# Rotating images by 90 degrees: one queue with all loads before all stores, larger load packets, and a slab parked in PSUM

## The chip, the cores and the metric

One core of a Trainium2 chip; the other cores are idle. The metric is device time in microseconds (us) of one execution, as the median of several runs. The spread of a kernel's runs is mostly 0.1 to 0.3%, and the verdict of "faster" or "slower" asks for 2%.

Ratios are the mean time of one kernel's fast runs over the mean time of the other's fast runs of the same rounds on the same chip, so they are not quite the ratio of the medians that are quoted beside them.

## The reference

A batch of 32 images with 3 channels, each plane 256 x 256 in fp32, is turned clockwise by 90 degrees. Nothing is computed: 25.17 MB go in, 25.17 MB come out.

```python
def setup_inputs():
    batch, c, h, w = 32, 3, 256, 256
    return {"x": np.random.randn(batch, c, h, w).astype(np.float32)}

def reference(x):
    return np.rot90(x, k=-1, axes=(-2, -1)).astype(np.float32)
```

## The kernel before

The 96 planes are cut into 24 slabs of 1 MB (4 planes). A partition holds 8 rows of a plane, which are 8 KB in one piece of memory. VectorE transposes blocks of 32 x 32; the access patterns put the reversed rows in their places. SyncE issues the loads, ScalarE the stores, each on its own DMA queue. Twelve input and twelve output buffers let both run at once. The first two stores are cut into packets of 2 KB, all other packets have 8 KB (a packet is what has a record of its own in the trace: a load of 1 MB in rows of 8 KB has 128 of them, a store of 1 MB in pieces of 2 KB has 512).

```python
    R = 8
    G = H // R
    n_slabs = B * C * G // P
    SHORT = 2
    ld_v = x.rearrange("b c h w -> (b c h) w").rearrange("(n p r) w -> n p (r w)", p=P, r=R)
    st_v = out.rearrange("b c h w -> (b c h) w").rearrange("(n p c) w -> n p (c w)", p=P, c=R)
    # ... pools of 12 buffers each ...
    for n in range(n_slabs):
        t_in = in_pool.tile([P, R * W], fp32, tag="t_in")
        nc.sync.dma_start(out=t_in, in_=ld_v[n])
        t_out = out_pool.tile([P, R * W], fp32, tag="t_out")
        src = t_in.rearrange("p (r g c) -> p c r g", r=R, c=R)
        dst = t_out.rearrange("p (c g r) -> p c r g", c=R, r=R)[:, :, ::-1, ::-1]
        parts = 2 if n in (0, n_slabs - 1) else 1
        for k in range(parts):
            cs = slice(k * R // parts, (k + 1) * R // parts)
            nc.vector.transpose(out=dst[:, cs], in_=src[:, cs])
        nc.scalar.dma_start(out=st_v[n], in_=t_out,
                            max_dma_last_dim=2048 if n < SHORT else 8192)
```

## Time and profile before

| | before |
|---|---|
| time | 124.11 us (124.02 to 124.44, 3 runs); with the later rounds 124.23 us (6 runs) |
| span in the profile | 122.4 us |
| bytes moved by DMA | 50.33 MB |
| first to last data packet | 119.4 us |
| VectorE busy | 91.6 us |

The lines of the page. The first gives busy us, share of the span and instructions of each engine. "DVE" (VectorE) and "DMA" give the busy share in tenths for 40 equal slices, "GB/s" the bytes moved in each slice.
```profile
DVE 91.6 (75%) x26; POOL 0.2 (0%) x4
...
DVE  0199999999999999999999999697796793000000
...
DMA  2999999999999999999999999999999999999994
GB/s 83 426 428 428 390 428 424 422 421 426 424 428 418 428 426 420 426 428 428 426 428 428 428 428 428 428 426 426 428 428 428 426 428 428 428 428 426 428 428 193
```

DMA is at 9 from the second slice to the last but one, and moves 420 to 428 GB/s nearly always: DMA bounds the kernel. VectorE does nothing in the last six slices.

The table by stretches (stretch in us from the start of the span, its length, busy us of VectorE and GpSimd with their instructions, clock of TensorE, busy share of DMA, GB/s):

```profile
core 0: us, DVE busy (x) POOL busy (x), PEclk, DMA share, GB/s
...
4.00:9.00 5.00, 3.35 (x2) 0.00 (x0) 1.00 1.01 428
...
12.00:15.00 3.00, 3.00 (x2) 0.00 (x0) 1.00 1.02 399
...
40.00:56.00 16.00, 16.00 (x5) 0.00 (x0) 1.00 1.01 427
...
59.00:63.00 4.00, 4.00 (x2) 0.00 (x0) 1.00 1.01 426
...
98.00:120.00 22.00, 3.98 (x2) 0.00 (x0) 1.00 1.01 428
```

From 4 to 9 us there are only loads, from 40 to 56 us loads and stores mixed, from 98 to 120 us only stores: 427 or 428 GB/s for all three.

The main group of VectorE's transpositions (line, engine, operation, tiles, shapes, count, then busy us and mean ns of one, then idle time before them and what ended it), and its last two in the timeline (start, us, ...):

```profile
L53 DVE STREAM_TRANSPOSE t_out<-t_in 128x2048 f32<-128x2048 f32 x22 | 83.8, 3936 | 3.8 <-DMA t_in<-in_x_dram 3.8
```

```profile
98.08 3.98 DVE L53 STREAM_TRANSPOSE t_out<-t_in 128x1024 f32<-128x1024 f32 x2 [0.99 <-DMA t_in<-in_x_dram]
```

A transposition of 2048 elements per partition takes 3.94 us. The last ends at 102.1 us, 20 us before the end of the span.

The trace also has a record of each DMA packet. Of these I use the time that a packet took, and the mean distance of packet starts on one engine, worked out from bytes and rate:

```
packet    took      start to start
 8 KB     309 ns    306.6 ns  (427.5 GB/s over 16 engines)
 2 KB      84 ns     81 ns
```

### The profile page before, as it was taken

What the parts mean: (1) busy time and instruction counts of PE and PEld (TensorE: products, weight loads), DVE (VectorE), ACT (ScalarE), POOL (GpSimd) and SP (SyncE); (2) the same over time, 40 slices, a digit from 0 to 9 for tenths busy, and PEclk for the clock granted to TensorE, in tenths of its full rate; (3) what the DMA queues carried; (4) which work ended last, traced back from release to release, by engine and by line L of the source; (5) the groups of instructions that cost most, each with busy time, mean ns of one, the idle gap of its engine ahead of it and who ended that gap; (6) DMA issues with size and microseconds to landing.
All of it is one profiled execution on the core that took longest, in us unless ns stands there. A gap on an engine that the chain in (4) does not pass through costs nothing.

```text
span 122.4 us, 164 instructions
## 1 busy us (share of the span) xinstructions
DVE 91.6 (75%) x26; POOL 0.2 (0%) x4
## 2 busy tenths in 40 slices
DVE  0199999999999999999999999697796793000000
POOL 0000000000000000000000000000000000000000
DMA  2999999999999999999999999999999999999994
GB/s 83 426 428 428 390 428 424 422 421 426 424 428 418 428 426 420 426 428 428 426 428 428 428 428 428 428 426 426 428 428 428 426 428 428 428 428 426 428 428 193
DMA packets 7680, 50.33 MB, mean 411 GB/s; under 512 B 768, under 2 KB 768, under 8 KB 1792
## 3 DMA queue, kind: packets, MB, share of 16 engines
q1 hardware_dynamic: 3456, 25.17, 49.1%
q10 hardware_dynamic: 4224, 25.17, 49.0%
HBM read 25.17 MB, written 25.17 MB: 411 GB/s over the span
## 4 chain that ended last, share of the span: by engine, by line
DMA 78%; DVE 2%; DVEq 2%; SPq 1%; issue 0%
DMA t_in<-in_x_dram 78%; DVE t_out L53 2%; DVEq L82 2%; SPq L45 1%; DVEq L53 0%
## 5 line engine op out<-in xcount | busy, mean ns | idle before, releaser
L53 DVE STREAM_TRANSPOSE t_out<-t_in 128x2048 f32<-128x2048 f32 (+1 forms) x26 | 91.6, 3647 | 10.4 <-DMA t_in<-in_x_dram 10.4
L71 POOL MEMSET const-bfloat16-1.0<- 128x1 bf16 x1 | 0.1, 102 | 0.0
L71 POOL MEMSET const-uint8-127<- 128x1 uint8 x1 | 0.1, 102 | 0.0
L71 POOL MEMSET const-float32-0.0<- 128x1 f32 x1 | 0.1, 99 | 0.2 <-issue 0.2
L71 POOL MEMSET const-float32-1.0<- 128x1 f32 x1 | 0.1, 99 | 0.0
## 6 DMA issues: line engine op xcount, KB each, us to landing
t_in<-in_x_dram SPq DMA_DIRECT2D x24, 1024.0 KB, 14.4
out_dram<-t_out ACTq DMA_DIRECT2D x24, 1024.0 KB, 19.5
```

The source lines that it names most:

```text
L45: nc.sync.dma_start(out=t_in, in_=ld_v[n])
L53: nc.vector.transpose(out=dst[:, cs], in_=src[:, cs])
L71: nc = _bacc.Bacc("TRN2", target_bir_lowering=False, num_devices=1)
L82: with _tile.TileContext(nc) as tc:
```

## The change

The intent: fewer and larger load packets, one queue that first loads everything and then stores everything, and no buffers beyond the input itself. Twelve units of 2 MB in SBUF hold the whole input (16 KB per partition each). Slab n, turned, goes into the unit that slab n-1 has left; slab 0 goes into PSUM and is copied into the last unit by ScalarE when all is turned. In slabs 1 to 10 a partition holds 16 rows (16 KB in one piece); a load fills every second partition with the first four planes of the slab, a second load the others. Slab 1's store is split into 128 KB (1 KB packets), 896 KB (7 KB packets) and 1 MB.

```diff
+    RI, RO = 16, 8
+    K = H // RI
+    I = 2
+    Q = P // (K * I)
     # ...
+    ld8_v = rows_in.rearrange("(n i p r) w -> n p i (r w)", i=I, p=P, r=RO)
+    ld16_v = rows_in.rearrange("(n i m r) w -> n i m (r w)", i=I, m=Q * K, r=RI)
+    st_v = rows_out.rearrange("(n i p c) w -> n p i (c w)", i=I, p=P, c=RO)
     # ...
     for n in range(n_slabs):
-        t_in = in_pool.tile([P, R * W], fp32, tag="t_in")
-        nc.sync.dma_start(out=t_in, in_=ld_v[n])
+        if n == last:
+            nc.sync.dma_start(out=units[n], in_=ld8_v[n])
+            continue
+        for i in range(I):
+            if n == 0:
+                nc.sync.dma_start(out=units[n][:, i], in_=ld8_v[n][:, i])
+            else:
+                nc.sync.dma_start(out=units[n][i::I].rearrange("p i f -> p (i f)"), in_=ld16_v[n, i])
     # ...
+    for n in range(n_slabs):
+        t_in, t_out = units[n], units[n - 1] if n else turned0
     # ... slabs 0 and 11 are turned as before, the others so:
+            src = t_in.rearrange("p i f -> p (i f)").rearrange("p (r g c) -> p c r g", r=RI, c=RO)
+            dst = t_out.rearrange("p i (c k r) -> p c r k i", c=RO, r=RI)[:, :, ::-1, ::-1, :]
+            for h in range(2):
+                cs = slice(h * RO // 2, (h + 1) * RO // 2)
+                nc.vector.transpose(out=dst[:, cs], in_=src[:, cs])
-        nc.scalar.dma_start(out=st_v[n], in_=t_out,
-                            max_dma_last_dim=2048 if n < SHORT else 8192)
+        if n == 1:
+            nc.sync.dma_start(out=st_v[n][:, 0, :W], in_=t_out[:, 0, :W])
+            nc.sync.dma_start(out=st_v[n][:, 0, W:], in_=t_out[:, 0, W:])
+            nc.sync.dma_start(out=st_v[n][:, 1], in_=t_out[:, 1])
+        elif n:
+            nc.sync.dma_start(out=st_v[n], in_=t_out)
+    for i in range(I):
+        nc.scalar.copy(out=units[last][:, i], in_=turned0[:, i])
+    nc.sync.dma_start(out=st_v[0], in_=units[last])
```

More of the change, by code (lines that the diff above doesn't have):

```diff
@@ L31 @@
     P = nc.NUM_PARTITIONS
-    R = 8
-    G = H // R
-    n_slabs = B * C * G // P
-    SHORT = 2
-    ld_v = x.rearrange("b c h w -> (b c h) w").rearrange("(n p r) w -> n p (r w)", p=P, r=R)
-    st_v = out.rearrange("b c h w -> (b c h) w").rearrange("(n p c) w -> n p (c w)", p=P, c=R)
-    in_pool = ctx.enter_context(tc.tile_pool(name="in_pool", bufs=12))
-    out_pool = ctx.enter_context(tc.tile_pool(name="out_pool", bufs=12))
-    for n in range(n_slabs):
-        t_in = in_pool.tile([P, R * W], fp32, tag="t_in")
-        nc.sync.dma_start(out=t_in, in_=ld_v[n])
-        t_out = out_pool.tile([P, R * W], fp32, tag="t_out")
-        src = t_in.rearrange("p (r g c) -> p c r g", r=R, c=R)
-        dst = t_out.rearrange("p (c g r) -> p c r g", c=R, r=R)[:, :, ::-1, ::-1]
-        parts = 2 if n in (0, n_slabs - 1) else 1
-        for k in range(parts):
-            cs = slice(k * R // parts, (k + 1) * R // parts)
-            nc.vector.transpose(out=dst[:, cs], in_=src[:, cs])
-        nc.scalar.dma_start(out=st_v[n], in_=t_out,
-                            max_dma_last_dim=2048 if n < SHORT else 8192)
+    RI, RO = 16, 8
@@ new lines @@
+    K = H // RI
+    I = 2
+    Q = P // (K * I)
+    n_slabs = B * C // (Q * I)
+    last = n_slabs - 1
+    F = RO * W
+    rows_in = x.rearrange("b c h w -> (b c h) w")
+    rows_out = out.rearrange("b c h w -> (b c h) w")
+    ld8_v = rows_in.rearrange("(n i p r) w -> n p i (r w)", i=I, p=P, r=RO)
+    ld16_v = rows_in.rearrange("(n i m r) w -> n i m (r w)", i=I, m=Q * K, r=RI)
+    st_v = rows_out.rearrange("(n i p c) w -> n p i (c w)", i=I, p=P, c=RO)
+    pools = [ctx.enter_context(tc.tile_pool(name=f"unit{u}", bufs=1)) for u in range(n_slabs)]
@@ new lines @@
+    units = [pool.tile([P, I, F], fp32, name=f"u{u}") for u, pool in enumerate(pools)]
+    psum = ctx.enter_context(tc.tile_pool(name="psum", bufs=1, space=bass.MemoryType.PSUM))
+    turned0 = psum.tile([P, I, F], fp32, name="turned0")
+    for n in range(n_slabs):
+        if n == last:
[6 more added lines that the diff above has]
+                nc.sync.dma_start(out=units[n][i::I].rearrange("p i f -> p (i f)"), in_=ld16_v[n, i])
@@ new lines @@
+    for n in range(n_slabs):
+        t_in, t_out = units[n], units[n - 1] if n else turned0
+        if n in (0, last):
+            for i in range(I):
+                src = t_in[:, i].rearrange("p (r g c) -> p c r g", r=RO, c=RO)
+                dst = t_out[:, i].rearrange("p (c g r) -> p c r g", c=RO, r=RO)
+                nc.vector.transpose(out=dst[:, :, ::-1, ::-1], in_=src)
+        else:
+            src = t_in.rearrange("p i f -> p (i f)").rearrange("p (r g c) -> p c r g", r=RI, c=RO)
[9 more added lines that the diff above has]
+            nc.sync.dma_start(out=st_v[n], in_=t_out)
@@ L60 @@
+    for i in range(I):
+        nc.scalar.copy(out=units[last][:, i], in_=turned0[:, i])
+    nc.sync.dma_start(out=st_v[0], in_=units[last])
 _INS = ['x']
```

## The prediction

> **What bounds the kernel now.** The DMA engines. In the page's slices they are 90% busy or more from the second slice to the second last, mostly at 428 GB/s; the table by stretches gives 428 GB/s for 4 to 9 us (loads only), 40 to 95 us (mixed) and 98 to 120 us (stores only): direction and mixing cost nothing. 50.33 MB at 428 GB/s is 117.6 us of the 122.4 us span. The rest is 2 us before the first packet, slow first packets (307 GB/s from 2 to 4 us), the final drain, and 14 to 34 us at 423 GB/s. VectorE is busy 91.6 us and not the limit: DMA stores for 20 us after its last transposition (102 us).
>
> **What a packet costs.** In the trace's packet records an 8 KB packet takes 309 ns (306.6 ns start to start per engine), a 2 KB packet 84 ns (about 81). The line through both is 36.7 ns per KB plus 5.8 ns per packet.[...]
>
> **What the change does to DMA.**
> - 20 of 24 MB of loads go from 8 KB to 16 KB packets: 80 fewer per engine, x 5.8 ns = 0.46 us saved.
> - Two stores leave 2 KB packets: 48 fewer per engine, 0.28 us saved. One store split into 1 KB and 7 KB: 0.05 us lost.
> - Bytes, start and drain stay. Separating loads from stores saves nothing.
> Sum: 0.7 us, all on the critical path.
>
> **What it does to VectorE.** 24 pieces of 3.94 us remain: 94.5 us from 5.7 us on, so it ends near 101 us; two ScalarE copies from PSUM follow[...]. Loads end near 60 us; slab n (2 MB, 4.9 us) is stored from 60 + 4.9(n-1), and turned by 5.7 + 7.9(n+1). Slab 1: turned at 21 us, wanted at 60; slab 11: 101 and 109; slab 0: copied by 104, wanted at 114. VectorE stays hidden, by about 8 us, unless a piece grows by over 9%. One queue suffices: an issue takes 0.4 us against 2.4 us of transfer.
>
> **Predicted: 123.4 us, range 122.4 to 125.2.** Faster by over 2%: 0.05; within 2%: 0.81; slower by over 2%: 0.14.
>
> **What would show each step.** 16 KB packets near 607 ns start to start, loads at 431 GB/s; stores at 427 to 428; DMA at 9 in all slices, no gap near 60 us. Transpositions near 3.9 us, the last done by 102 us, none late in the chain of waits.
>
> **What would make it wrong.**
> 1. Loads go to every second partition, 64 at a time.[...] No run shows it yet.
> 2. Turned elements are written alternately 8 KB apart, and slab 0 into PSUM. If a piece takes over 4.3 us, the last slabs are late for their stores, DMA idles near 105 us, and the time grows by about 0.95 us per further 1%.
> 3. The turn from loads to stores in one queue leaves a bubble of over 1 us.
> A gain over 2% would need the ends (4 us) to shrink, which nothing here does.

0.46 + 0.28 - 0.05 is about 0.7 us, each from the 5.8 ns per packet that its line through the 8 KB and 2 KB packets gives (80, 48 and 8 packets). The 104 us for slab 0 rests on a guess of mine for the time of a copy from PSUM; it took 1.87 us.

## The result, and the profile after

| | before | after |
|---|---|---|
| time | 124.23 us (124.0 to 124.44, 6 runs) | 123.98 us (123.92 to 124.17, 6 runs) |
| ratio | | 0.9983, 95% interval 0.9967 to 0.9998 |
| span in the profile | 122.4 us | 122.2 us |
| first to last data packet | 119.43 us | 119.08 us |

The same kernel run again as a control on the chip of the first experiments gave 123.96 us, ratio 0.9976 (0.9964 to 0.9988). So the gain is 0.2 to 0.3 us, where 0.7 us was forecast. The time lies inside the stated range; the change is "within 2%", as forecast; but the gain is about a third of its forecast size. The stated range is 2.8 us wide and holds the time of the kernel before as well, so that it was met says little.

The same lines of the page, after:

```profile
DVE 93.3 (76%) x24; ACT 5.0 (4%) x3; POOL 0.2 (0%) x4
...
DVE  0299999999999999999999999999999940000000
...
DMA  3999999999999999999999999999999999999993
GB/s 88 429 432 434 440 440 429 429 429 429 429 429 429 429 429 424 434 424 408 370 414 428 426 429 429 429 429 429 429 429 429 424 429 429 429 429 426 429 429 166
```

DMA is at 9 throughout here too, and over a quarter of the packets is gone (the page counts 7680 before, 5584 after). The slices that matter are the 19th to 21st: 408, 370, 414 GB/s. They lie at 55 to 64 us, where the one queue turns from loads to stores.

The table by stretches (now with a column for ScalarE). Rates of short stretches wobble where packets are 16 KB (436 GB/s from 4 to 9 us, 419 from 9 to 14 us), so that 436 is not a rate above the others:

```profile
core 0: us, DVE busy (x) ACT busy (x) POOL busy (x), PEclk, DMA share, GB/s
...
4.00:9.00 5.00, 3.50 (x1) 0.00 (x0) 0.00 (x0) 1.00 1.03 436
...
12.00:15.00 3.00, 2.97 (x2) 0.00 (x0) 0.00 (x0) 1.00 1.02 437
...
40.00:56.00 16.00, 15.93 (x5) 0.00 (x0) 0.00 (x0) 1.00 1.00 426
...
59.00:63.00 4.00, 3.96 (x2) 0.64 (x1) 0.00 (x0) 1.00 0.99 372
...
98.00:120.00 22.00, 1.22 (x1) 1.87 (x1) 0.00 (x0) 1.00 1.01 428
```

From 59 to 63 us only 372 GB/s moved, against 426 in the kernel before. In exchange the dip at 12 to 15 us is gone, since no store enters there. From 40 to 56 us, loads alone run at 426 GB/s in this view (428 over the longer stretch of 25 to 58 us, where the wobble weighs less) and not at the 431 that the packet size promised.

Was the turn late because the stores were late? The timeline of SyncE's queue shows the issues of the first stores (start, us, ...):

```profile
42.28 0.36 SPq L85 DMA_DIRECT2D out_dram<-u  x1
...
49.60 0.38 SPq L89 DMA_DIRECT2D out_dram<-u  x1
```

No. The first store was in the queue at 42.3 us, 19 us before its first packet moved (61.4 us by the packet records). The records show one thing more: the loss is in the loads, and it comes before any store packet moves. The first 8 KB loads over 340 ns start at 59.3 us, 2 us ahead of the first store packet. In the kernel before, the first such load where the stores enter starts at 12.4 us and the first store packet at 13.3 us.

VectorE's groups and its end:

```profile
L82 DVE STREAM_TRANSPOSE u<-u 128x2048 f32<-128x2048 f32 x20 | 78.0, 3948 | 0.3
...
L76 DVE STREAM_TRANSPOSE turned<-u 128x2048 f32<-128x2048 f32 x2 | 7.6, 3828 | 5.5 <-DMA u<-in_x_dram 5.5
L92 ACT COPY u<-turned 128x2048 f32<-128x2048 f32 x2 | 3.7, 1866 | 33.8 <-DVE u L76 33.8
```

```profile
91.47 7.75 DVE L76 STREAM_TRANSPOSE u<-u 128x2048 f32<-128x2048 f32 x2
...
99.26 1.87 ACT L92 COPY u<-turned 128x2048 f32<-128x2048 f32 x1 [1.93 <-DVE u L76]
101.15 0.37 SPq L93 DMA_DIRECT2D out_dram<-u  x1
```

A transposition takes 3.95 us, as before, also where its output alternates between places 8 KB apart; into PSUM it takes 3.83 us. The last one ends at 99.2 us, the last store is issued at 101.2 us, and DMA has stores to do until then and 15 us beyond. This part of the prediction (VectorE hidden by about 8 us, one queue enough) held.

What the packet records say of the loads: a 16 KB packet took 611 ns in every case until about 21 us into the span; then more and more took 613 to 622 ns, with a mean of 614 ns from 25 us on. From the first to the last of the 80 packets of an engine the distance of starts was 610.6 ns on average (608.5 in the first third, 611.6 in the last). Two 8 KB packets of the kernel before took 613.2 ns.

### The profile page after: what moved, and what is told of

Same layout as the page of the kernel before. It is cut to its first block, busy times and chain, and to the rows that moved or that the text cites. A ratio compares the mean times of both kernels' runs of the same rounds, so it can differ in the third digit from the quotient of the medians.

```text
span 122.2 us, 134 instructions
## 1 busy us (share of the span) xinstructions
DVE 93.3 (76%) x24; ACT 5.0 (4%) x3; POOL 0.2 (0%) x4
## 2 busy tenths in 40 slices
DMA packets 5584, 50.33 MB, mean 412 GB/s; under 512 B 592, under 2 KB 720, under 8 KB 848
## 3 DMA queue, kind: packets, MB, share of 16 engines
q1 hardware_dynamic: 5584, 50.33, 97.8%
## 4 chain that ended last, share of the span: by engine, by line
DMA 57%; DVE 13%; issue 7%; DVEq 3%; ACT 2%; SPq 1%
DMA u<-in_x_dram 39%; DMA out_dram<-u 18%; DVE u L82 10%; DVE u L76 3%; DVEq L119 3%; ACT u L92 2%; SPq L66 1%; SPq L89 0%
## 5 line engine op out<-in xcount | busy, mean ns | idle before, releaser
L82 DVE STREAM_TRANSPOSE u<-u 128x2048 f32<-128x2048 f32 x20 | 78.0, 3948 | 0.3
L76 DVE STREAM_TRANSPOSE turned<-u 128x2048 f32<-128x2048 f32 x2 | 7.6, 3828 | 5.5 <-DMA u<-in_x_dram 5.5
L76 DVE STREAM_TRANSPOSE u<-u 128x2048 f32<-128x2048 f32 x2 | 7.8, 3953 | 0.0
L92 ACT COPY u<-turned 128x2048 f32<-128x2048 f32 x2 | 3.7, 1866 | 33.8 <-DVE u L76 33.8
## 6 DMA issues: line engine op xcount, KB each, us to landing
u<-in_x_dram SPq DMA_DIRECT2D x22, 1024.0 KB, 19.6
out_dram<-u SPq DMA_DIRECT2D x1, 128.0 KB, 20.6
```

The costliest lines, as they stand in the source:

```text
L76: nc.vector.transpose(out=dst[:, :, ::-1, ::-1], in_=src)
L92: nc.scalar.copy(out=units[last][:, i], in_=turned0[:, i])
```

## The experiments

The turn is the place where a queue goes from loads to stores. To compare turns, I work out a loss from the packet records. A line through the undisturbed packets (8 KB 306.1 ns start to start, 16 KB 607.4) gives 4.75 ns per packet plus 36.79 ns per 1000 bytes. The loss of a stretch is its length less the time that the bytes in it need by that line on 16 engines. It counts what an engine loses, whatever the reason. This is the loss in the 3 to 5 us around the place where stores first enter (16 us for a2_two_queues), with the longest load or store packet there, from one execution of each kernel. Two executions of the changed kernel (after and a1_control) differ by 0.14 us, so smaller differences in this table say nothing:

```
                                            packets: load, first store   loss us   longest ns
kernel before          two queues             8 KB       2 KB            0.21       538
b4_before_8k           two queues             8 KB       8 KB            0.84       698
c4_before_1k           two queues             8 KB       1 KB            0.06       408
kernel after           one queue             16, 8 KB    1 KB            0.45       775
a1_control             one queue             16, 8 KB    1 KB            0.31       587
a4_no_split            one queue             16, 8 KB    8 KB            0.39       658
b1_last16              one queue             16 KB       1 KB            0.36      1107
b2_no_dve              one queue             16, 8 KB    1 KB            0.52       778
b3_early_store (turn)  one queue             16, 8 KB    7 KB            0.36       556
c3_first_store_2k      one queue             16 KB       2 KB            0.25      1006
d1_last2_8k            one queue             16, 8 KB    1 KB            0.23       561
d2_last4_8k            one queue             16, 8 KB    1 KB            0.22       660
c2_16_then_8           one queue             16, 8 KB    1 KB            0.04       338
a3_load8k              one queue              8 KB       1 KB            0.05       338
c1_load8k_nosplit      one queue              8 KB       8 KB            0.02       321
a2_two_queues          two queues            16 KB       1 KB            2.20      1753
```

My first theory: the gain was lost in two places, at the turn (the stores' entry into engines that still load) and in the long stretch of loads alone, whose packets go from 611 to 614 ns. The rival: a larger packet saves less than I worked out.

### a1_control: the changed kernel once more

No edit. 

> The changed kernel once more, as the control for the other runs on this chip. Both theories: 0.2 to 0.35 us under the kernel before. If the losses seen in its first trace are properties of the kernel, they recur: DMA under 400 GB/s for some 1.5 us at the turn from loads to stores (about 0.45 us lost), and 16 KB load packets that go from 611 ns each to a mean of 614 ns about 22 us into the span (about 0.2 us lost). If they are accidents of one execution, they are absent or elsewhere.

Measured: 123.96 us, ratio 0.9976 (0.9964 to 0.9988). Both losses recur in this second execution, so they belong to the kernel: 16 KB packets that go from 611 to 614 ns, and 0.31 us at the turn, where the first execution had 0.45.

### a2_two_queues: stores on ScalarE's queue

```diff
-            nc.sync.dma_start(out=st_v[n], in_=t_out)
+            nc.scalar.dma_start(out=st_v[n], in_=t_out)      # and so for all stores
```

> The changed kernel with its stores issued from ScalarE, so that loads (16 KB packets) and stores (8 KB) interleave and the turn of one queue is gone. Theory T (what was missing in the gain is lost at the turn and in the long stretch of loads alone): the dip at the turn shrinks to that of the kernel before (about 0.15 us), the 16 KB packets stay at 611 ns, and it is 0.3 to 0.5 us faster than the control, 0.6 to 0.8 us under the kernel before. Rival R (the saving per packet was over-estimated): same time as the control within 0.15 us.

Measured: 127.99 us (127.28 to 128.85, 6 runs), ratio 1.0306 (1.0273 to 1.0339). A clear miss: I expected it faster and it was the slowest of all. Slices and groups show why:

```profile
DVE  0299999999999999407999949939949933990000
...
GB/s 95 436 459 413 413 454 413 334 396 328 358 449 423 415 425 438 431 410 444 426 413 433 438 418 446 415 426 459 405 418 436 426 420 438 425 150 286 415 413 206
```

```profile
L82 DVE STREAM_TRANSPOSE u<-u 128x2048 f32<-128x2048 f32 x20 | 78.0, 3950 | 11.6 <-DMA u<-in_x_dram 11.4
L76 DVE STREAM_TRANSPOSE u<-u 128x2048 f32<-128x2048 f32 x2 | 7.7, 3951 | 4.1 <-DMA u<-in_x_dram 4.1
```

The entry of stores, now at about 20 us, costs 2.2 us (the slices with 334 to 358 GB/s): the dip is not a matter of one queue. Then VectorE waits for loads (11.4 us in 5 waits before its main group, 4.1 us before the last), is late, and DMA runs dry near 113 us (the slice with 150). That stores take a share of the engines from the loads is seen in the trace of the kernel before, where both queues moved about equal numbers of packets: with 8 KB loads against 2 KB stores (20 to 34 us) 569 and 619, so that the loads moved 333 GB/s and the stores 90; with 8 KB on both sides (40 to 56 us) 417 each, 214 GB/s each. So "all loads first" is what lets VectorE run through, and that is worth more in this kernel than its larger packets.

### a3_load8k: loads in 8 KB packets

```diff
-                nc.sync.dma_start(out=..., in_=ld16_v[n, i])
+                nc.sync.dma_start(out=..., in_=ld16_v[n, i], max_dma_last_dim=8192)
```

> The changed kernel with the loads of slabs 1 to 10 in 8 KB packets. If the cost per packet is 5.8 ns as predicted, it is 0.46 us slower than the control; if the late slowing of the loads eats half of the saving at 16 KB and would not hit 8 KB packets, only 0.2 us slower; under rival R (larger packets save nothing) equal to the control within 0.1 us.

Measured: 124.21 us, ratio 0.9998 (0.9986 to 1.001); 0.25 us slower than the control. So 16 KB packets do help, against the rival, but the number hides two opposite things. Loads alone at 8 KB slow down earlier and more: from 15 us on the packets take 313.5 ns on average instead of 309 (422 GB/s). And the dip at the turn is absent: 0.05 us. Its slices show both (the turn is in the 20th and 21st):

```profile
GB/s 91 425 428 428 425 425 415 420 423 423 425 428 415 420 420 423 425 423 428 417 412 428 431 425 431 428 425 431 425 428 428 428 431 425 428 428 428 428 428 193
```

### a4_no_split: slab 1's store in one piece

```diff
-        if n == 1:
-            ...three stores...
-        elif n:
+        if n:
             nc.sync.dma_start(out=st_v[n], in_=t_out)
```

> The changed kernel with slab 1's store as one 2 MB transfer instead of 128 KB in 1 KB packets, 896 KB and 1 MB. By packet cost 0.05 us faster than the control. If the dip at the turn is caused by the 1 KB packets, it goes, and the gain is 0.3 to 0.45 us; if the dip is caused by the turn itself, it stays, and perhaps grows where the split was meant to soften it.

Measured: 123.9 us, ratio 0.9979 (0.9966 to 0.9992), not to be told from the control. The dip stays at 0.39 us, so the 1 KB packets are not its cause.

### b1_last16: the last slab in 16 KB packets too

```diff
-        if n == last:
-            nc.sync.dma_start(out=units[n], in_=ld8_v[n])
-            continue
     # ...
-        if n in (0, last):
+        if n == 0:
```

> The changed kernel with its last slab loaded and turned like slabs 1 to 10, so that 16 KB packets run right up to the turn. By packet cost 0.04 us faster. Theory T1 (the dip is the entry of stores into engines that still load): the dip stays, 0.3 to 0.5 us, and the time is that of the changed kernel (123.9 to 124.0). Rival T2 (the dip comes from the change of packet size, 16 KB to 8 KB, which the run with 8 KB loads throughout did not have and which showed no dip): no dip, and 0.3 to 0.4 us faster than the changed kernel, near 123.6.

Measured: 123.8 us (123.79 to 123.98), ratio 0.9963 (0.9951 to 0.9975). The dip stays at 0.36 us: the change of packet size ahead of the turn isn't its cause. It is the lowest median.

### b2_no_dve: no VectorE work (wrong result)

```diff
-                nc.vector.transpose(out=dst[:, :, ::-1, ::-1], in_=src)
+                pass                                   # both transpositions, and the PSUM copies
```

> Wrong result on purpose: the changed kernel without its transpositions and PSUM copies; the same loads and stores in the same order. If VectorE's writes into SBUF disturb the loads, the 16 KB packets stay at 611 ns throughout and the dip at the turn is gone: 0.5 us faster than the changed kernel. If loads disturb each other[...], the packets slow from 611 to 614 ns about 22 us into the span as before, the dip stays, and the time is within 0.15 us of the changed kernel.

Measured: 124.1 us, ratio 0.9981 (0.9968 to 0.9994). Without any engine at work the 16 KB packets still go from 611 to 614 ns at the same time, and the turn costs 0.52 us, as its stretch shows (columns as for the kernel after, without VectorE and ScalarE; 372 GB/s there):

```profile
59.00:63.00 4.00, 0.00 (x0) 1.00 1.01 366
```

VectorE has no part in either loss, and it is nowhere on the path that sets the time.

### b3_early_store: 128 KB stored in mid-load

```diff
+    # the first 128 KB of slab 1 are stored between the loads of slabs 7 and 8
+    nc.sync.dma_start(out=st_v[1][:, 0, :W], in_=units[0][:, 0, :W])
     # ... loads of slabs 8 to 11, then the other stores as before
```

> The changed kernel with the first 128 KB of slab 1 stored in mid-load, ahead of the load of slab 8. If the dip is a cost of the first stores of an execution, it moves there (near 42 us) and the turn has none; time unchanged. If it is a cost of each turn from loads to stores, there are now two dips and the time is up to 0.4 us longer. If it needs a long stretch of loads behind it, the small one in mid-load also resets the drift, and 16 KB packets after it are at 611 ns again.

Measured: 124.18 us, ratio 0.9991 (0.9977 to 1.0006). The small store cost 0.06 us where it ran, and the turn 0.36 us as ever. So the dip is not paid once per execution. As the third expectation had it, the 16 KB packets right behind the small store were back at 611 ns for some 5 us, and then slowed again. What slows them is not shown.

### b4_before_8k: the kernel before without its 2 KB packets

```diff
-    SHORT = 2
+    SHORT = 0
```

> The kernel before with its first two stores in 8 KB instead of 2 KB packets, all else as it was. By the predicted 5.8 ns per packet it is 0.28 us faster than the kernel before. Rival: the 2 KB packets gave the loads a larger share of the engines early on, which filled the input buffers; then the saving is given back, and the time is the same within 0.1 us or longer.

Measured: 124.31 us, ratio 1.0001 (0.9989 to 1.0013): the predicted 0.28 us did not come. The stretches of this run (columns as for the kernel before):

```profile
12.00:15.00 3.00, 3.00 (x2) 0.00 (x0) 1.00 1.00 339
15.00:20.00 5.00, 5.00 (x2) 0.00 (x0) 1.00 1.01 426
```

The stretch of 12 to 15 us has fallen from 399 to 339 GB/s. The packets saved their 0.2 us, and the entry of stores grew from 0.21 to 0.84 us. VectorE's waits for loads, of no cost here, doubled as the rival foresaw (from 10.4 to 20.6 us). In the sum the two still should leave a loss of 0.4 us, which the profiled execution has (119.7 us from first to last packet, against 119.4) and the median of the runs does not; the entry's size is known from one execution only.

### c4_before_1k: the kernel before with 1 KB packets

```diff
-                            max_dma_last_dim=2048 if n < SHORT else 8192)
+                            max_dma_last_dim=1024 if n < SHORT else 8192)
```

> The kernel before with its first two stores in 1 KB instead of 2 KB packets. If smaller store packets soften their entry among loads, the loss there falls below the 0.2 us of 2 KB packets (8 KB: 0.8 us), against 0.27 us for 64 more packets per engine: 124.3 to 124.5. If size does not matter and the difference between 2 and 8 KB was chance, the loss is anywhere from 0.2 to 0.8 us.

Measured: 124.04 us, ratio 0.9988 (0.9972 to 1.0004). The entry cost 0.06 us. So with two queues, smaller store packets soften the stores' entry: 0.84, 0.21 and 0.06 us for 8, 2 and 1 KB, one execution each. The time forecast, 124.3 to 124.5 us, did not come: 64 more packets per engine are 0.3 us by the line above and the entry saved 0.15, yet the median fell; the packet records put a further 0.13 us into a shorter drain at the end, from one execution.

### c1_load8k_nosplit: 8 KB loads, and slab 1's store in one piece

The edits of a3 and a4 together.

> The changed kernel with 8 KB loads throughout and slab 1's store as one transfer in 8 KB packets. It asks what set the dip at the turn to nearly nothing in the run with 8 KB loads. If loads of 8 KB suffice, no dip here either (under 0.1 us), and a time near 124.2. If small store packets are needed beside 8 KB loads (as the kernel before showed: 0.2 us lost at the entry of 2 KB stores, 0.8 us at the entry of 8 KB stores), a dip of 0.4 to 0.8 us and a time of 124.5 to 124.9.

Measured: 124.13 us, ratio 0.9991 (0.9978 to 1.0003). No dip (0.02 us). The size of the first store packets made no difference here: 0.02 us with 8 KB, 0.05 us with 1 KB (a3), one execution each.

### c2_16_then_8: 16 KB for slabs 1 to 5, then 8 KB

```diff
+                                  max_dma_last_dim=16384 if n < 6 else 8192)
```

> The changed kernel with 16 KB packets for slabs 1 to 5 and 8 KB packets for slabs 6 to 11. If the dip goes where loads come in 8 KB packets for long before the turn, no dip, and by packets 0.2 us lost against the changed kernel, 0.35 us won: about 123.8. If the dip is set by something else that 16 KB packets left behind[...], it stays, and the time is about 124.2.

Measured: 123.96 us, ratio 0.9979 (0.9967 to 0.9991).

```profile
40.00:56.00 16.00, 15.93 (x5) 0.00 (x0) 0.00 (x0) 1.00 1.02 424
59.00:63.00 4.00, 3.96 (x2) 0.62 (x1) 0.00 (x0) 1.00 1.01 414
```

The dip is gone (414 GB/s from 59 to 63 us, of which 128 KB in 1 KB packets; 0.04 us by the packet records), and the time is that of the changed kernel, as 8 KB loads give the difference back.

### c3_first_store_2k: b1 with slab 1's store in 2 KB packets

```diff
+            for i in range(I):
+                nc.sync.dma_start(out=st_v[n][:, i], in_=t_out[:, i], max_dma_last_dim=2048)
```

> The kernel with 16 KB loads up to the turn, slab 1's store now wholly in 2 KB packets (2 MB instead of 128 KB of small packets). If a longer stretch of small store packets softens the turn as it did in the kernel before, the dip falls from 0.36 to about 0.2 us or less, against 0.2 us for 48 more packets per engine: 123.8 again. If it does nothing, 124.0.

Measured: 124.02 us (123.77 to 124.32), ratio 0.9986 (0.997 to 1.0002). The dip was 0.25 us, the packets cost 0.2 us; no gain.

### d1_last2_8k and d2_last4_8k: how long a stretch of 8 KB loads

```diff
-                                  max_dma_last_dim=16384 if n < 6 else 8192)
+                                  max_dma_last_dim=16384 if n < 10 else 8192)     # d1; n < 8 in d2
```

> The changed kernel with 8 KB packets for slabs 10 and 11, 16 KB for slabs 1 to 9. If the last few microseconds of loads decide, no dip, and 123.65 us (0.3 us under the changed kernel). If the loads need a longer stretch at 8 KB, as I suspect since one slab did not do it, the dip of 0.3 to 0.5 us stays and the time is that of the changed kernel, 123.95.

> 8 KB packets for slabs 8 to 11. If 20 us of 8 KB loads are enough, no dip and 123.75 us. If not, a dip and 124.05.

Measured: 123.87 us, ratio 0.9973 (0.9961 to 0.9986), and 123.85 us, ratio 0.9963 (0.9952 to 0.9975). The dip is 0.23 and 0.22 us: not gone as with six slabs of 8 KB. Whether it is smaller than with one slab (0.45 and 0.31 us in two executions) one execution each does not settle.

### d3_alternate_16k and d4_alternate_8k: six turns instead of one

```diff
+    for n in range(6, n_slabs):      # loads of slabs 0 to 5 come first, alone
+        load(n)
+        turn(n)
+        store(n - 5)                 # slabs 1 to 6, each queued behind a load
+    for n in range(7, n_slabs):
+        store(n)
```

> The changed kernel with the stores of slabs 1 to 6 each queued behind the load of slabs 6 to 11, so that the one queue turns six times from loads to stores and five times back, all else equal. If each turn behind 16 KB loads costs 0.3 to 0.5 us, it is 1.2 to 2 us slower than the changed kernel (125.2 to 126), with six dips in the trace. If the loss comes once per execution, or only behind a long stretch of loads, one dip and 123.7 to 124.

> The same alternation with 8 KB loads throughout. If turns behind 8 KB loads cost nothing by themselves, no dips, and as the loads have no long stretch to drift in, 123.9 to 124.1, under the run with 8 KB loads and one turn (124.2). If the freedom from dips needed the drift, that is the slowed state of loads at 313 ns, dips appear here too, and it is 124.8 to 126.

Measured: 126.09 us, ratio 1.0147 (1.0134 to 1.016), and 125.94 us (125.17 to 126.58), ratio 1.0129 (1.0103 to 1.0154). Stretches of d3 (columns as for the kernel after):

```profile
32.00:50.00 18.00, 17.93 (x6) 0.00 (x0) 0.00 (x0) 1.00 0.98 397
50.00:95.00 45.00, 44.79 (x12) 1.28 (x1) 0.00 (x0) 1.00 1.01 426
...
120.00:124.30 4.30, 0.00 (x0) 0.00 (x0) 0.00 (x0) 1.00 0.27 114
```

By the packet records the six turns from loads to stores cost 0.75, 0.32, 0.01, 0.09, 0.15 and 0.03 us in d3, and 0.27, 0.26, 0.14, 0.01, 0.04 and 0.08 us in d4 (stretches of 4 or 5 us). The five turns back from stores to loads cost at most 0.01 us each. The very end takes the rest: from 116 us on, 1.6 us are lost in both runs, against 0.33 in the kernel after. Some engines finish later than the others there (in d3 four of the 16 still move data at 122 us, when the rest are done), so the engines did not lose the same, and the last of them is waited for. Turns thus differ widely in cost, and no price per turn can be read from this. The first turn of d4 is telling: it comes behind 36 us of 8 KB loads alone, slowed to 313 ns as in a3, and it costs 0.27 us where a3's cost 0.05. So the freedom from loss in a3, c1 and c2 comes neither from 8 KB packets alone nor from a long, slowed stretch of them.

### e1_drain_first and e2_drain_all: no store in the queue while loads run (wrong results on purpose)

e1: the last slab's store was put first, in the kernel without VectorE. e2: every store takes the last slab loaded as its source.

```diff
-        t_in, t_out = units[n], units[n - 1] if n else turned0
+        t_in, t_out = units[n], units[last]          # e2
```

> Wrong result on purpose: the run without VectorE once more, but the store of the last slab comes first, so that no store can be issued before the last load has landed. If stores standing behind the loads cause the slow loads at the turn (8 KB loads of up to 778 ns in the run without VectorE), the last loads now stay at 309 to 321 ns;[...] the time is near 126.5. If the end of the loads is slow by itself, packets of 400 to 700 ns appear there again.

> Wrong result on purpose: no VectorE work, and every store takes the last slab loaded as its source, so that no store at all is issued before the last load has landed. If stores standing behind the loads cause the slow loads before the turn, the last loads stay at 309 to 321 ns;[...] the time is about 126.5. If the end of the loads is slow by itself, packets of 400 to 700 ns appear there again, without any store near them.

e1 measured 124.35 us and answers nothing: two stores of slab 1 (1 MB) were issued at 42 and 45 us all the same, ahead of the one meant to hold them back, and the dip was there (0.30 us). One thing in it is unexplained: its stores slowed from 309 to 314 ns late in the run, which no other run with ordinary stores showed.

e2 measured 126.53 us, ratio 1.0189 (1.0172 to 1.0206), as expected; the forecast time rested on an estimate of mine for how long DMA stands still. What SyncE waited for before its first store, and the stretches around the turn (columns as before, without VectorE):

```profile
SPq L85 <- DMA u<-in_x_dram: 21.6, 2, 19.6
```

```profile
58.00:60.00 2.00, 0.00 (x0) 1.00 0.97 406
60.00:62.00 2.00, 0.00 (x0) 1.00 0.59 246
62.00:64.00 2.00, 0.00 (x0) 1.00 0.62 238
```

SyncE waits 19.6 us for the load, no store stands in the queue, and by the packet records every 8 KB load takes 309 to 321 ns to the very last one, which starts at 61.1 us. Then DMA stands still for about 1.4 us: SyncE issues the first store at 61.95 us, and the first store packet starts at 62.8 us. In b2, with stores in the queue and no VectorE work either, the same loads took up to 778 ns. So, by one traced execution each, the slow loads ahead of the turn come only when stores stand behind them in the queue.

## Why the prediction was right or wrong

**Right.** DMA bounds both kernels. The transpositions took 3.95 us against 3.94 predicted, VectorE's work ended at 99.2 us (101 predicted), the last store was issued at 101.2 us, some 15 us before its turn (its 2 MB end near 121 us and take 4.9 us), one queue sufficed, no engine other than DMA is on the path (b2: no VectorE work, no faster). Loads into every second partition, the first thing feared, were not slow: they ran at 431 GB/s in their first third (608.5 ns start to start, 16 KB packets). The bubble of over 1 us at the turn did not come either, but a smaller one did.

**Wrong: the sum of 0.7 us and its reading "all on the critical path".** Its terms against the profiles before and after:

| term | predicted us | measured us | from |
|---|---|---|---|
| 80 fewer load packets per engine | -0.46 | -0.21 | 80 x (613.2 - 610.6 ns) |
| 48 fewer store packets per engine | -0.28 | -0.23 | 48 x 4.75 ns |
| the split store | +0.05 | +0.04 | 8 x 4.75 ns |
| the turn in place of the stores' entry | 0 | +0.24 | 0.45 - 0.21 (+0.10 with the control's 0.31) |
| first packets, drain, pure stores at 428.0 instead of 427.5 GB/s | 0 | about -0.17 | packet records, 0.08, 0.02 and 0.07 |
| sum | -0.70 | about -0.33 | |

From first to last packet the two profiles differ by 0.35 us, so the account closes within a tenth; the times differ by 0.2 to 0.3 us. Part of this is luck: nobody forecast the 0.17 us of the last term, and the 0.08 us of its first packets did not recur (the control lost 0.10 us more there than the kernel before).

- The step that failed first: "Bytes, start and drain stay. Separating loads from stores saves nothing." It saves nothing, but it is not free. It rested on "direction and mixing cost nothing", read from stretches that left the stores' entry out, though my own table had 410 GB/s from 9.6 to 14 us. The kernel before paid 0.21 us where stores entered among its loads, the changed one pays 0.3 to 0.5 us at its turn. The loss needs stores that stand in the queue behind loads: in e2, without them, the loads ran undisturbed to the end, in b2, with them, they did not. Such stores are not enough for it, as a3, c1 and c2 had them and lost under 0.1 us. It is not VectorE (b2), the small packets (a4), the change of packet size (b1), or a cost of the first store of an execution (b3, d3).
- "16 KB packets near 607 ns start to start, loads at 431 GB/s" held for the first third (608.5 ns). Later packets took 614 ns instead of 611. The slowing comes without VectorE (b2), comes sooner and stronger with 8 KB packets (313.5 instead of 309 ns), and was undone for some 5 us by a small store in between (b3). The cost per packet was mis-sized too: 4.75 ns from 8 and 16 KB packets, and not 5.8, which leaves 0.38 of the 0.46 us; the slowing takes the other 0.17. I had taken a rate from the five microseconds of loads alone that the kernel before has, for a stretch of 58 us.
- "Two stores leave 2 KB packets: 0.28 us saved." The packets do save 0.23 us by the line above, but b4 got nothing from it: in the kernel before, small store packets keep the stores' entry cheap (0.21 us against 0.84 with 8 KB and 0.06 with 1 KB). A cost counted as pure overhead was paying for something.

**Open.** What the loads and the stores behind them contend for is not shown. Why a turn behind a long stretch of 8 KB loads cost almost nothing in three kernels, and 0.27 us at the first turn of d4, isn't either. That turn differs from theirs in two ways, which no run takes apart: more loads stand behind its stores, and the last slab ahead of it went to every second partition. Nor is it shown why the loads slow down with time.

The lowest median is that of the changed kernel with 16 KB packets also in the last slab (b1): 123.8 us, ratio 0.9963 to the kernel before; d2 has the same ratio at 123.85 us. Against the changed kernel the difference of the ratios, 0.9963 to 0.9976 and 0.9983, is as large as the intervals, so b1 beats the kernel before (by 0.4%), and the changed kernel only by the median.

## What to carry to other kernels

Where DMA was busy all the time, as here, larger packets were worth tenths of a microsecond (0.21 us for the loads, 0.23 for the stores), and the place where loads and stores first meet was worth as much (0.02 to 0.84 us in the table of losses, a2 with its 2.2 us left out): read the packet times there before you count on a saving per packet. Breaking up "all loads first" in the changed kernel cost far more, 2 us (d3, d4) and 4 us (a2). A rate read in a short stretch need not hold in a long one of the same kind (16 KB loads: 431 GB/s in the first third, 428 from 25 to 58 us). An odd-looking setting in a tuned kernel, like two stores in small packets, should be taken out by itself first, since it may be paying for something that its own cost does not show.
